# A gate product that keeps its place in program order on VectorE

## The chip, the core and the metric

The kernel runs on one core of a Trainium2 chip. A core has five engines that run their own instruction queues: TensorE (PE in the profile, its weight loads PEld), VectorE (DVE), ScalarE (ACT), GpSimd (POOL) and SyncE (SP). The metric is the device time of one launch in microseconds; lower is better.

## What is computed

The reference is one decoder layer on x of 512 tokens by 1024 channels, in float32: a mixer (projections, two causal convolutions, a linear recurrence, gates), and then a feed-forward part that picks, for every token, 16 of 16384 experts per head with 8 heads. Only the second part touches the change:

```python
def peer(n, w_q, sub_keys_1, sub_keys_2, expert_u, expert_v):
    ...
        g = jax.nn.softmax(top_s, axis=-1)
        u_sel = jnp.take(expert_u, idx, axis=0)
        act = jax.nn.gelu(jnp.einsum('thkd,td->thk', u_sel, xc).astype(jnp.float32))
        v_sel = jnp.take(expert_v, idx, axis=0)
        return jnp.einsum('thk,thkd->td', (g * act).astype(xc.dtype), v_sel)
    ...
    h = h + peer(n, w_q[l], sub_keys_1[l], sub_keys_2[l], expert_u[l], expert_v[l])
    return rms_norm(h, norm_final)
```

## The kernel before, in words

For 384 of the 512 tokens the kernel does not gather experts. It computes gelu(U n) for all 16384 experts, in 128 tiles of 128 experts, multiplies each tile by a dense matrix of gates (zero where an expert was not chosen), and accumulates the product with V in PSUM. The last 128 tokens go by gathered rows: 128 indirect DMAs, each bringing one expert row (u and v) per token, with two VectorE instructions each (L410 for the dot product, L397 for the sum).

Every matmul is done in three passes with high and low parts. A weight tile of 128x1024 is loaded on SP's queue (`raw`, 4 buffers), ScalarE rounds it into `whi` (L75) and VectorE subtracts to get `wlo` (L76).

The stages are: the mixer, the search for the top experts, the building of the gate matrix (written to a DRAM scratch `gscr`), and last the expert stage, the loop over j from 0 to 128 at the end of `layer`. The change touches only that last stage.

An activation tile comes from one of two places. 52 of the 128 tiles are computed in the loop itself by `act_tile` (24 matmuls, L90; the gelu at L378 writes tile `gel`). The other 76, listed in `LAG`, were computed in earlier stages: 12 of them wait in SBUF (`keep`), 64 were written to DRAM (`ascr`) and are read back in the loop (`back`, 6 buffers) by DMAs on ScalarE's queue (L673), requested three tiles ahead.

`out_tile(j, g)` then does, for the tile before the current one: reads of gates for the next eight tiles (`gt`, two buffers, four DMAs per group of eight tiles on ScalarE's queue, L637); the load and the splitting of V (`weights`); the product of activations and gates on VectorE (L650); the splitting of that product into `w_hi` (ScalarE, L75) and `w_lo` (VectorE, L76), two buffers each; and 18 matmuls (L657), in which `w_hi` times `whi` comes first, `w_hi` times `wlo` second, and `w_lo` times `whi` third.

What sets the order on each engine is a scheduler in the framework: it takes the instructions in the order in which they become ready by its own estimate, within the limits of buffers and data. A call of `tc.keep_in_program_order` takes an instruction out of that freedom: it stays in the written order among all others so marked. Marked already are the two VectorE instructions of a gathered row and the DMAs of `gt` and `back`. Within an engine the built order is then fixed, and each instruction starts only when the one before it has started and its own waits are over.

Of the kernel before, what the change touches and what calls it, by code (L numbers as in the profile page):

```python
# [35 lines left out]
TG = 32  # L36
# [20 lines left out]
def layer(ctx: ExitStack, tc: tile.TileContext, a):  # L57
    nc = tc.nc
    V, A, G, T, SP = nc.vector, nc.scalar, nc.gpsimd, nc.tensor, nc.sync
# [12 lines left out]
    def split(raw, shape, tags, pool, bufs, lo_eng=None):  # L72
        hi = pool.tile(shape, F32R, tag=tags[0], name=tags[0], bufs=bufs)
        lo = pool.tile(shape, F32R, tag=tags[1], name=tags[1], bufs=bufs)
        A.activation(hi, raw, AF.Copy)  # L75
        (lo_eng or V).tensor_sub(lo, raw, hi.bitcast(F32))  # L76
        return hi, lo

    def weights(src, k, eng=None):
        raw = ring.tile([P, k * P], F32, tag="raw", name="raw", bufs=4)  # L80
        SP.dma_start(raw, src)
        hi, lo = split(raw, [P, k * P], ("whi", "wlo"), ring, 3, eng)
        return hi.rearrange("p (k m) -> p k m", k=k), lo.rearrange("p (k m) -> p k m", k=k)
# [65 lines left out]
    with tc.tile_pool(name="mix", bufs=1) as mp:  # L149
# [64 lines left out]
        for j in range(KR):  # L214
# [16 lines left out]
            c = next(columns)  # L231
            held[c] = proj(c, COLS)
            gates = []
            for s, bname, tag in ((0, "brg", "lr"), (1, "big", "lx")):
# [3 lines left out]
                gt = mp.tile([P, S], F32, tag=tag, name=tag, bufs=KR)  # L238
# [131 lines left out]
    def act_tile(j):  # L370
        u = weights(a["ut"][j], KD, G if j in LAG[:AR + AD] else V)
        pa = bank("01", (P, S))
        mm3(pa[:, :ND], u, n2d)
        if j in LAG[:JK]:
            g = gp.tile([P, ND], F32, tag="keep", name="keep", bufs=JK)
        else:
            g = gp.tile([P, ND], F32, tag="gel", name="gel", bufs=3)
        A.activation(g, pa[:, :ND], AF.Gelu_apprx_tanh)  # L378
        return g
# [42 lines left out]
    with tc.tile_pool(name="top", bufs=1) as rp:  # L422
# [114 lines left out]
        for t in range(NT):  # L537
            g, sel = decode(t)
# [13 lines left out]
    with tc.tile_pool(name="gates", bufs=1) as rp:  # L552
# [19 lines left out]
        for n, (t, t0) in enumerate(blocks):  # L572
# [3 lines left out]
            c, s0 = divmod(t0, TG)  # L576
# [54 lines left out]
    def read_gates(n, c0, c1):  # L631

        if n * JG >= P:
            return
        if c0 == 0:
            gst[n] = ep.tile([P, NG, JG, TG], F32, tag="gt", name="gt", bufs=2)
        tc.keep_in_program_order(A.dma_start(gst[n][:, c0:c1], gscr[c0:c1, :, n * JG : (n + 1) * JG, :].rearrange("c p j t -> p c j t")))  # L637

    def out_tile(j, g):
        nonlocal nout  # L640
        k = j % JG
        if j == 0:
            for c in range(0, NG, 2):
                read_gates(0, c, c + 2)
        if 3 <= k < 7:
            read_gates(j // JG + 1, 3 * k - 9, 3 * k - 6)
        gt = gst[j // JG][:, :, k, :]
        v = weights(a["uv"][j * P : (j + 1) * P, D:], KD, V)
        vf = [x.rearrange("p k m -> p (k m)") for x in v]
        V.tensor_mul(g.rearrange("p (c t) -> p c t", t=TG), g.rearrange("p (c t) -> p c t", t=TG), gt)  # L650
        w = split(g, [P, ND], ("w_hi", "w_lo"), ep, 2)
        passes = [(x, y, f) for x, y in ((0, 0), (0, 1), (1, 0)) for f in range(2)]
        if nout == P - 1:
            passes.sort(key=lambda p: p[2])
        for t in range(NT):
            for x, y, f in passes:
                T.matmul(  # L657
                    acc[t][f],
                    w[x][:, t * P : (t + 1) * P],
                    vf[y][:, f * S : (f + 1) * S],  # L660
                    start=nout == 0 and (x, y) == (0, 0),
                    stop=nout == P - 1 and (x, y) == (1, 0),
                    skip_group_check=True,
                )
        nout += 1
# [17 lines left out]
    for j in range(P + 1):  # L683
        if j < P:
            read_back(j + PRE)
            g = kept[j] if j in LAG else act_tile(j)
            part += share[j]
        if prev is not None:
            out_tile(*prev)
        if 8 <= j < 8 + 2 * KD and j % 2 == 0:  # L690
            residual(j // 2 - 4)
        prev = (j, g)
        while done < min(len(work), math.ceil(part * len(work) / total)):
            work[done]()
            done += 1
# [54 lines left out]
```

## Time and profile before

| | |
|---|---|
| median of 3 runs | 1806.83 us (1806.39 to 1808.25) |
| the profiled execution | 1811.19 us |
| its span, first to last instruction | 1809.5 us |
| PE busy in the span | 1738.8 us |
| VectorE busy in the span | 1287.9 us |
| expert stage, 1012 to 1797 us | 785 us, PE busy 753.37 us |

The profile is one execution, so sums are made against its span. Idle time of an engine counts only where the end waits for it. In the rows further down a PE row with brackets names how long PE stood idle before it, and what it was released by.

### The profile page before, as it was taken

The page shows a single profiled execution, that of the slowest core. Times are in us where ns is not written, and L with a number is a line of the kernel's source. Part 1 is how long each engine was busy: PE and PEld are TensorE (multiplying, and loading weights), DVE is VectorE, ACT ScalarE, POOL GpSimd, SP SyncE. Part 2 cuts the span into 40 slices and gives each one's busy share as a digit, 9 for nine tenths or more (in the row PEclk, how much of TensorE's full clock was granted, in tenths as well). Part 3 has the DMA queues.
Part 4 walks back from the last instruction along what each step waited for, and adds up shares of the span by engine and source line. Part 5 has one row for each costly group of instructions (what it writes and reads, how often), then busy time and mean ns, then how long its engine had stood idle before and what let it go on. Part 6 is the DMA issues. An engine that isn't in the chain of part 4 may idle for free. (4 is left out here: it accounts for less than half of the span.)

```text
span 1809.5 us, 23987 instructions
## 1 busy us (share of the span) xinstructions
PE 1738.8 (96%) x8861; PEld 1515.1 (84%) x8861; DVE 1287.9 (71%) x2341; ACT 765.6 (42%) x1290; POOL 386.9 (21%) x257
## 2 busy tenths in 40 slices
PE   8999999999989998999999899999899999989998
PEld 6888888888878887999999788888787887878886
DVE  8969442225578669999996676777777876767774
ACT  5774332222343336455554333443333433434353
POOL 0000000000145555022685112122121221112200
PEclk9999999999999999999999999999999999999999
DMA  4323223333433335589999897898898897878872
GB/s 167 125 79 103 94 86 93 102 105 99 138 105 103 105 119 195 168 319 370 351 361 372 308 324 275 324 356 318 287 331 307 320 335 274 333 280 315 308 238 90
DMA packets 124246, 410.85 MB, mean 227 GB/s; under 512 B 12128, under 2 KB 55392, under 8 KB 106080
## 3 DMA queue, kind: packets, MB, share of 16 engines
q1 hardware_dynamic: 59904, 199.58, 33.1%
q0 software_dynamic: 18432, 134.23, 19.2%
q10 hardware_dynamic: 45792, 75.51, 11.5%
q8 instruction: 69, 1.13, 0.2%
q14 instruction: 49, 0.40, 0.1%
HBM read 367.33 MB, written 41.94 MB: 226 GB/s over the span
## 5 line engine op out<-in xcount | busy, mean ns | idle before, releaser
L75 ACT ACTIVATE whi<-raw 128x1024 fp32r<-128x1024 f32 (+1 forms) x364 | 380.1, 1046 | 601.5 <-PE ps L90 388.3
L76 DVE TENSOR_TENSOR wlo<-raw,whi 128x1024 fp32r<-128x1024 f32 (+1 forms) x324 | 387.9, 1199 | 237.0 <-ACT whi L75 236.5
L90 PE MATMUL ps<-q_hi,whi 128*128 128x384 f32 (+1 forms) x1232 | 435.5, 353 | 14.6 <-ACT whi L75 10.3
L90 PE MATMUL ps<-q_hi,wlo 128*128 128x384 f32 (+1 forms) x1232 | 429.5, 349 | 2.0 <-DVE wlo L76 2.0
L90 PE MATMUL ps<-q_lo,whi 128*128 128x384 f32 (+1 forms) x1232 | 429.0, 348 | 0.3 <-DVE q_lo L144 0.3
L403 POOL DMA_INDIRECT row<-uv,uidx x128 | 262.9, 2054 | 716.9 <-DVE yg L397 712.2
L657 PE MATMUL acc<-whi,w_hi 128*128 128x512 f32 x768 | 245.3, 401 | 29.7 <-ACT w_hi L75 25.4
L90 PEld LDWEIGHTS ps<-q_hi,whi 128*128 128x128 f32 x1232 | 234.3, 190 | 27.4 <-ACT whi L75 11.6
L657 PE MATMUL acc<-whi,w_lo 128*128 128x512 f32 x768 | 243.3, 398 | 6.2 <-DVE w_lo L76 6.2
L90 PEld LDWEIGHTS ps<-q_hi,wlo 128*128 128x128 f32 x1232 | 233.5, 190 | 13.8 <-DVE wlo L76 4.8
L90 PEld LDWEIGHTS ps<-q_lo,whi 128*128 128x128 f32 x1232 | 234.1, 190 | 10.9 <-DVE q_lo L144 0.7
L657 PE MATMUL acc<-wlo,w_hi 128*128 128x512 f32 x768 | 242.3, 397 | 0.0
L657 PEld LDWEIGHTS acc<-whi,w_hi 128*128 128x128 f32 x768 | 145.7, 193 | 62.3 <-ACT w_hi L75 31.7
L657 PEld LDWEIGHTS acc<-whi,w_lo 128*128 128x128 f32 x768 | 147.5, 193 | 39.3 <-DVE w_lo L76 7.9
L76 POOL TENSOR_TENSOR wlo<-raw,whi 128x1024 fp32r<-128x1024 f32 x40 | 98.5, 2466 | 357.1 <-ACT whi L75 357.1
L657 PEld LDWEIGHTS acc<-wlo,w_hi 128*128 128x128 f32 x768 | 147.2, 192 | 32.0
L90 PE MATMUL ps<-n_hi,whi 128*128 128x512 f32 x432 | 168.4, 390 | 0.0
L90 PE MATMUL ps<-n_hi,wlo 128*128 128x512 f32 x432 | 168.2, 390 | 0.0
L90 PE MATMUL ps<-n_lo,whi 128*128 128x512 f32 x432 | 168.1, 389 | 0.0
L397 DVE SCALAR_TENSOR_TENSOR yg<-row,dots,yg 128x1024 f32<-128x1024 f32 x128 | 163.5, 1278 | 0.0
L410 DVE SCALAR_TENSOR_TENSOR junk<-row,n2tok 128x1024 bf16<-128x1024 f32 x128 | 155.6, 1216 | 0.0
L90 PEld LDWEIGHTS ps<-n_hi,wlo 128*128 128x128 f32 x432 | 81.1, 188 | 17.5 <-DVE wlo L76 0.4
(204 smaller groups left out, 1902.0 us busy)
## 6 DMA issues: line engine op xcount, KB each, us to landing
raw<-ut SPq DMA_DIRECT2D x128, 512.0 KB
raw<-uv SPq DMA_DIRECT2D x128, 512.0 KB
raw<-w_in SPq DMA_DIRECT2D x60, 512.0 KB
gscr<-stg ACTq DMA_DIRECT2D x12, 2048.0 KB
gt<-gscr ACTq DMA_DIRECT2D x60, 384.0 KB
ascr<-gel ACTq DMA_DIRECT2D x64, 192.0 KB
back<-ascr ACTq DMA_DIRECT2D x64, 192.0 KB
raw<-w_q SPq DMA_DIRECT2D x16, 512.0 KB
```

The lines of the kernel that those rows point to most:

```text
L75: A.activation(hi, raw, AF.Copy)
L76: (lo_eng or V).tensor_sub(lo, raw, hi.bitcast(F32))
L90: T.matmul(ps, w[x][:, i, :], r[y][i], start=first and n == 0, stop=last and n == 3 * k - 1)
L397: V.scalar_tensor_tensor(yg, r[:, D:], dots[:, i : i + 1], yg, op0=ALU.mult, op1=ALU.add)
L403: ins = G.indirect_dma_start(out=r, out_offset=None, in_=a["uv"], in_offset=bass.IndirectOffsetOnAxis(ap=uidx[:, i : i + 1], axis=0))
L410: V.scalar_tensor_tensor(junk, r[:, :D], 1.0, n2tok, op0=ALU.mult, op1=ALU.mult, accum_out=dots[:, i : i + 1])
L657: T.matmul(acc[t][f], w[x][:, t * P : (t + 1) * P], vf[y][:, f * S : (f + 1) * S], start=nout == 0 and (x, y) == (0, 0), stop=nout == P - ...
```

## The change

The product moves two lines up, ahead of `weights` for V of the same tile, and is marked to keep its place in program order.

```diff
         gt = gst[j // JG][:, :, k, :]
+        gv = g.rearrange("p (c t) -> p c t", t=TG)
+        tc.keep_in_program_order(V.tensor_mul(gv, gv, gt))
         v = weights(a["uv"][j * P : (j + 1) * P, D:], KD, V)
         vf = [x.rearrange("p k m -> p (k m)") for x in v]
-        V.tensor_mul(g.rearrange("p (c t) -> p c t", t=TG), g.rearrange("p (c t) -> p c t", t=TG), gt)
         w = split(g, [P, ND], ("w_hi", "w_lo"), ep, 2)
```

No instruction is added or removed. The order of PE, POOL and SP stays the same but for line numbers; VectorE and ScalarE are reordered within the expert stage. In the rows, `wlo` belongs to a weight tile, `w_lo` to a product; the product is L650 before and L649 after.

VectorE, before, around tile 42 (`gel_11506`) of the 128; `back_11544` is the activation of tile 46:

```order
L76 TENSOR_TENSOR w_lo_11516<-back_11297,w_hi_11515 128x384
L410 SCALAR_TENSOR_TENSOR junk_11539,dots_3822<-row_11537,n2tok_3823 128x1024
L397 SCALAR_TENSOR_TENSOR yg_3824<-row_11468,dots_3822,yg_3824 128x1024
L76 TENSOR_TENSOR wlo_11549<-raw_11546,whi_11548 128x1024
L650 TENSOR_TENSOR back_11544<-back_11544,gt_11189 128x384
L76 TENSOR_TENSOR wlo_11580<-raw_11577,whi_11579 128x1024
L650 TENSOR_TENSOR gel_11506<-gel_11506,gt_11189 128x384
L76 TENSOR_TENSOR w_lo_11554<-gel_11506,w_hi_11553 128x384
```

The same place on VectorE after the change:

```order
L410 SCALAR_TENSOR_TENSOR junk_11539,dots_3822<-row_11537,n2tok_3823 128x1024
L397 SCALAR_TENSOR_TENSOR yg_3824<-row_11468,dots_3822,yg_3824 128x1024
L76 TENSOR_TENSOR wlo_11550<-raw_11547,whi_11549 128x1024
L76 TENSOR_TENSOR wlo_11581<-raw_11578,whi_11580 128x1024
L649 TENSOR_TENSOR gel_11506<-gel_11506,gt_11189 128x384
L76 TENSOR_TENSOR w_lo_11554<-gel_11506,w_hi_11553 128x384
L649 TENSOR_TENSOR back_11366<-back_11366,gt_11189 128x384
L76 TENSOR_TENSOR w_lo_11585<-back_11366,w_hi_11584 128x384
```

The product of tile 46 no longer stands ahead of that of tile 42 (it is 15 rows behind it now), and that of tile 43 stands directly ahead of its own `w_lo`.

VectorE, before, around tiles 94 (`gel_14110`), 95 (`back_13974`) and 96 (`back_14047`), which is the first of a new group of gates (`gt_14009`):

```order
L650 TENSOR_TENSOR gel_14110<-gel_14110,gt_13614 128x384
L76 TENSOR_TENSOR w_lo_14167<-gel_14110,w_hi_14166 128x384
L650 TENSOR_TENSOR back_14047<-back_14047,gt_14009 128x384
L76 TENSOR_TENSOR w_lo_14196<-back_13974,w_hi_14195 128x384
L410 SCALAR_TENSOR_TENSOR junk_14219,dots_3822<-row_14217,n2tok_3823 128x1024
```

The same place on VectorE after the change:

```order
L649 TENSOR_TENSOR gel_14110<-gel_14110,gt_13614 128x384
L76 TENSOR_TENSOR w_lo_14167<-gel_14110,w_hi_14166 128x384
L649 TENSOR_TENSOR back_13974<-back_13974,gt_13614 128x384
L76 TENSOR_TENSOR wlo_14229<-raw_14226,whi_14228 128x1024
L76 TENSOR_TENSOR w_lo_14196<-back_13974,w_hi_14195 128x384
L410 SCALAR_TENSOR_TENSOR junk_14219,dots_3822<-row_14217,n2tok_3823 128x1024
L397 SCALAR_TENSOR_TENSOR yg_3824<-row_14149,dots_3822,yg_3824 128x1024
L649 TENSOR_TENSOR back_14047<-back_14047,gt_14009 128x384
```

The product of tile 96 has moved behind the `w_lo` of tile 95 and behind the two instructions of a gathered row.

## Rows read from the trace of the kernel before

**Rows 1.** Page, part 1: engine, busy us (share), instructions.

```profile
PE 1738.8 (96%) x8861; PEld 1515.1 (84%) x8861; DVE 1287.9 (71%) x2341; ACT 765.6 (42%) x1290; POOL 386.9 (21%) x257
```

**Rows 2.** Windows: stretch, length, busy PE PEld DVE ACT POOL, PEclk, DMA share, GB/s.

```profile
1012.00:1797.00 785.00, 753.37 (x3536) 652.22 (x3537) 576.10 (x743) 314.25 (x566) 146.97 (x100) 0.98 0.83 298
1166.00:1222.00 56.00, 56.00 (x271) 49.15 (x271) 45.56 (x59) 23.85 (x44) 13.02 (x9) 1.00 0.93 341
```

**Rows 3.** Waits, 1012 to 1797: waiter <- releaser: us, times, longest.

```profile
DVE back L650 <- DMA back<-ascr: 43.3, 21, 4.7
...
PE acc L657 <- ACT w_hi L75: 25.4, 15, 2.9
DVE back L650 <- DMA gt<-gscr: 22.6, 5, 8.9
...
PE acc L657 <- DVE w_lo L76: 6.2, 3, 4.7
...
PE acc L657 <- issue: 4.4, 1, 4.4
```

**Rows 4.** Timeline of DVE around tile 42: start, us, instruction [idle before <-releaser].

```profile
1266.43 0.56 DVE L650 TENSOR_TENSOR back<-back,gt 128x384 f32<-128x384 f32 x1 [4.72 <-DMA back<-ascr]
1266.91 1.22 DVE L76 TENSOR_TENSOR wlo<-raw,whi 128x1024 fp32r<-128x1024 f32 x1
1268.04 0.55 DVE L650 TENSOR_TENSOR gel<-gel,gt 128x384 f32<-128x384 f32 x1
```

**Rows 5.** Timeline of ACT, the gelu of tile 42.

```profile
1263.14 0.47 ACT L378 ACTIVATE gel<-ps 128x384 f32<-128x384 f32 x1
```

**Rows 6.** Timeline of PE, seven of the eighteen stalls by operands.

```profile
1106.28 0.74 PE L657 MATMUL acc<-whi,w_hi 128*128 128x512 f32 x2 [2.67 <-ACT w_hi L75]
...
1269.20 1.22 PE L657 MATMUL acc<-whi,w_hi 128*128 128x512 f32 x2 [2.80 <-ACT w_hi L75]
...
1306.68 1.22 PE L657 MATMUL acc<-whi,w_hi 128*128 128x512 f32 x2 [2.88 <-ACT w_hi L75]
...
1364.67 1.22 PE L657 MATMUL acc<-whi,w_hi 128*128 128x512 f32 x2 [2.78 <-ACT w_hi L75]
...
1503.56 0.73 PE L657 MATMUL acc<-whi,w_hi 128*128 128x512 f32 x2 [2.78 <-ACT w_hi L75]
...
1600.91 1.22 PE L657 MATMUL acc<-whi,w_lo 128*128 128x512 f32 x2 [4.72 <-DVE w_lo L76]
...
1708.47 0.73 PE L657 MATMUL acc<-whi,w_hi 128*128 128x512 f32 x2 [2.08 <-ACT w_hi L75]
```

**Rows 7.** Timeline of DVE, tiles 56 to 61.

```profile
1356.14 1.49 DVE L650 TENSOR_TENSOR back<-back,gt 128x384 f32<-128x384 f32 x3 [3.40 <-issue]
...
1361.90 0.56 DVE L650 TENSOR_TENSOR back<-back,gt 128x384 f32<-128x384 f32 x1 [0.32 <-DMA back<-ascr]
```

**Rows 8.** Chain that ended last: start, us, what.

```profile
1378.85 8.17 PE acc L657 x36
...
1492.66 9.71 DMA gt<-gscr
...
1587.16 12.55 DMA gt<-gscr
```

**Rows 9.** Windows of 4 us behind two stalls, columns as in rows 2.

```profile
1268.00:1272.00 4.00, 2.80 (x7) 2.22 (x8) 3.41 (x7) 2.46 (x5) 0.00 (x0) 0.62 0.71 258
...
1600.00:1604.00 4.00, 3.09 (x7) 2.48 (x8) 4.00 (x6) 1.78 (x4) 0.53 (x1) 0.51 0.15 39
1604.00:1608.00 4.00, 4.00 (x14) 3.32 (x13) 4.00 (x6) 1.49 (x4) 1.15 (x1) 0.64 0.66 174
```

**Rows 10.** Timeline of DVE, tiles 45 and 46, where PE does not wait.

```profile
1286.54 0.56 DVE L76 TENSOR_TENSOR w_lo<-gel,w_hi 128x384 fp32r<-128x384 f32 x1 [0.59 <-ACT w_hi L75]
...
1290.49 0.56 DVE L76 TENSOR_TENSOR w_lo<-back,w_hi 128x384 fp32r<-128x384 f32 x1
```

**Rows 11.** Timeline of PE, the first matmuls of tile 45.

```profile
1287.22 0.62 PE L657 MATMUL acc<-whi,w_hi 128*128 128x512 f32 x2
```

## Prediction

> **What bounds the kernel now.** I read the page first, then the waits of the last stage, then the timelines around its stalls. PE is busy 96% of the span [rows 1], so what can be won is PE's idle time and what follows from it. In the expert stage, 1012 to 1797 us, PE is busy 753 of 785 us [rows 2]. The waits of that stage name the missing part [rows 3]: PE's matmuls L657 wait 15 times for `w_hi` (25.4 us), 3 times for `w_lo` (6.2 us), and once 4.4 us at the start of the stage, where the first gates are loaded. The last one stays: nothing there changes. The other 31.6 us are what the change can reach.
>
> Both `w_hi` and `w_lo` come from the product, and the product's engine stands still for DMAs: VectorE waits 21 times, 43.3 us in all, for `back`, and 5 times, 22.6 us, for `gt` [rows 3]. How that gets to PE is seen at tile 42. Its gelu begins at 1263.14 and takes 0.47 [rows 5]. But the product of tile 46 stands ahead on VectorE and waits 4.72 us for its `back` [rows 4]; tile 42's own product runs only at 1268.04, and PE stands idle 2.80 us until 1269.20 [rows 6]. Tile 46 is needed four tiles later. So a wait for data that nobody needs yet blocks, on an in-order queue, data that PE needs now.
>
> **What the change removes.** It puts each product behind all that VectorE must do for earlier tiles. In the built order no product of `back` or `keep` stands ahead of the product of an earlier tile, and PE's order is the same. A `back` tile then has its product asked for when its own tile is next, several tiles after its DMA was issued. So the waits for `back` should vanish from the path. I went through the 18 stalls by the product that waited ahead of them.
>
> - Four stalls are at the first tile of a group of gates which PE reaches straight after other product tiles: 2.67, 2.88, 2.78 and 2.08 us at 1106, 1306, 1503 and 1708 [rows 6]. Here the tile itself needs the gates that have not landed. The order doesn't help, since the gate reads keep their places on ScalarE. 10.4 us stay.
> - At 1364.67 there are 2.78 us [rows 6], partly for the same reason: VectorE stood still until 1356.14 for tile 56, the first of its group, and then had work queued up [rows 7]. Before, three products ran there (1.49 us) and later one more waited 0.32 and ran 0.48 (as the first row of [rows 4] holds up the second). After, two of the three (1.0) and the last with its wait (0.8) are elsewhere, but the `wlo` of tile 56, formerly done during the wait, now stands behind the product: 1.13, the distance of two rows of [rows 4]. 2.78 - 1.0 - 0.8 + 1.13 = 2.1 us stay.
> - The rest goes: 31.6 - 10.4 - 2.1 = 19.1 us. The largest is the 4.72 at 1600.91 [rows 6], where the product of tile 96, waiting for new gates, blocked the `w_lo` of tile 95 in the middle of tile 95's matmuls. After the change that `w_lo` is ahead of it, and PE has the rest of tile 95 and the 24 matmuls of an activation tile to do until it wants tile 96. The stall of 2.80 at 1269.20 is the second.
>
> **The clock behind the stalls.** Behind a long stall PE runs slow for a while: the granted clock is 0.62 in the 4 us from 1268, and 0.51 and 0.64 in the 8 us from 1600 [rows 9], against 1.00 in a stretch without a stall [rows 2]. [...] The work lost is (1 - 0.62) x 4 = 1.5 us at the first, (0.49 + 0.36) x 4 = 3.4 us at the second. Both stalls go, so 4.9 us come back. For the stalls that stay, and for the one at 1364, I credit nothing.
>
> **What it costs.** The product itself is no new work: 128 of them, 0.55 us each [rows 4], as before. What is new is that the product of a kept tile stands behind the two instructions of a gathered row and ahead of `w_lo`. In a stretch without stalls the `w_lo` of tile 45 starts at 1286.54 and that of tile 46 at 1290.49, 3.95 later, with a gathered row and a `wlo` between [rows 10]. With a product of 0.48 it is 4.43, against 4.09 that PE takes for a tile (8.17 for two, [rows 8]). But VectorE is ahead: `w_lo` of tile 45 starts 0.68 before PE's first matmul of that tile, at 1287.22 [rows 11], and PE uses `w_lo` only in the third pass, behind four matmuls, 0.9 us in. So the next `w_lo` ends at 1286.54 + 4.43 + 0.56 = 1291.53, and is wanted at 1287.22 + 4.09 + 0.9 = 1292.21. I take this at zero; PE's own work hides it with 0.7 us to spare. Its bounds are zero and the second rival.
>
> ScalarE's queue has `w_hi` in order too: a `w_hi` that waits for a later product holds up the `whi` and the DMA issues behind it. The scheduler moved those `w_hi` back by some places, and the gate reads stand where they stood but for one place at a time. I take zero.
>
> The faster pace also loads the DMA engines more. They are busy 0.83 of the stage, and 0.93 in a stretch without stalls [rows 2]; a gate read lands 9.7 us after its issue, once 12.55 [rows 8]. At the four group starts that stay a later landing is lost one for one. I take 0.5 us each, 2 us, with bounds of 0 and 3 us each (12.55 against 9.7).
>
> [...]
>
> **The sum.** 19.1 + 4.9 - 2 = 22 us. The span goes from 1809.5 to 1787.5; the execution, 1.7 us longer than its span, from 1811.2 to 1789.2; and since the median lies 4.4 us below the profiled execution, the median to 1784.8. I say 1785, 1.2% faster.
>
> **The rivals.**
>
> *Gates become the bound.* The stalls for `back` go, but loads bunch up and the gate reads land later: the four stalls grow by 3 us each, to 1795; and if some of the other group starts that PE now passes without waiting begin to stall as well, to about 1801. For it: DMA at 0.93 without stalls, and gate reads issued only some 10 us before they are used. Against it: most group starts have an activation tile of 24 matmuls ahead of them on PE.
>
> *Products just in time (slower).* Each of the 52 computed tiles is followed on PE by a tile whose product was ready long before. Now it is made within one tile of PE's time. If VectorE is late by more than the 0.7 us worked out above, every such place loses what the product adds, 0.55 us: 52 x 0.55 = 29 us against the 22 that are won, so 1785 + 29 = 1814. It decides at the first `w_lo` behind a computed tile. Against it: VectorE is busy 576 of 785 us in the stage [rows 2].
>
> *Nothing changes in sum.* The stalls are only moved: PE waits for the gates at the next group start for as long as it saved before, since the loads behind are no faster. That would be 1803 to 1810. Against it: the DMA engines are idle 17% of the stage [rows 2], after stalls most of all (0.15 of the time from 1600, [rows 9]).
>
> *More than I think.* Gate reads land earlier because VectorE frees buffers evenly: half of the 10.4 us and its slow clock go too, below 1776.
>
> **How the numbers follow.** Forecast, 1775 to 1795: 0.63. Gates become the bound, 1795 to 1803: 0.20. More than I think: 0.03. Nothing in sum: 0.06. Slower: 0.08. A measurement of this kernel tells about 0.2%, 3.6 us, from no change. So faster is 0.63 + 0.20 + 0.03 = 0.86, same 0.06, slower 0.08. The range of 8 in 10 takes the forecast with its bounds and most of the first rival: 1772 to 1801.
>
> **What would show it.** Right: VectorE's waits for `back` fall from 43 us to a few; PE's waits for `w_hi` and `w_lo` fall from 31.6 to about 13, and stand at the first tiles of groups; the granted clock no longer falls around tiles 42 and 95. Wrong: many short stalls of PE for `w_lo` behind computed tiles (the second rival), or waits for `gt` that grew past 30 us (the first).

## The result, and the profile after

| | before | after |
|---|---|---|
| median of 6 runs | 1809.38 us (1806.39 to 1814.81) | 1785.84 us (1781.47 to 1790.10) |
| the profiled execution | 1811.19 us | 1786.26 us |
| its span | 1809.5 us | 1784.5 us |

The ratio is 0.9867, 95% interval 0.9845 to 0.9889: the change is 1.3% faster. The forecast was 1785 us, in a range from 1772 to 1801.

VectorE does the same work in the same time (1287.9 us before, 1287.8 after). PE's busy time fell from 1738.8 [rows 1] to 1728.9 us, although it runs the same matmuls. Page of the changed kernel, part 1, columns as in rows 1:

```profile
PE 1728.9 (97%) x8861; PEld 1509.5 (85%) x8861; DVE 1287.8 (72%) x2341; ACT 764.2 (43%) x1290; POOL 325.2 (18%) x257
```

Nearly the whole difference lies in the expert stage: 24.2 of the 25.0 us by which the span is shorter. Windows from PE's first matmul of the stage to the end of the span, columns as in rows 2, first of the kernel before and then of the changed one:

```profile
1012.11:1809.50 797.39, 757.24 (x3552) 655.06 (x3552) 581.00 (x755) 320.02 (x581) 146.97 (x100) 0.98 0.82 295
```

```profile
1011.35:1784.50 773.15, 748.82 (x3552) 651.61 (x3552) 580.77 (x755) 318.89 (x581) 145.99 (x100) 0.98 0.85 304
```

Of the 24.2 us, 8.4 us are PE's busy time (757.24 - 748.82), and the remaining 15.8 us are its idle time. The waits say where the idle time went. Waits of the changed kernel from 1012 us to the end, which answer to [rows 3] (waiter <- releaser: us, times, longest):

```profile
DVE back L649 <- DMA gt<-gscr: 26.8, 6, 6.9
...
PE acc L658 <- ACT w_hi L75: 15.8, 7, 3.7
...
PE acc L658 <- issue: 4.8, 1, 4.8
DVE back L649 <- DMA back<-ascr: 2.2, 1, 2.2
```

VectorE's waits for `back` are down from 21 with 43.3 us to one with 2.2. PE waited 18 times, 31.6 us, for `w_hi` and `w_lo`, and now waits 7 times, 15.8 us, for `w_hi` alone; there is no row of PE waiting for `w_lo` any more. VectorE's waits for `gt` grew from 22.6 to 26.8 us, but most of that is a change of name: its wait at tile 56, the first of a group, stood under `issue` with 3.40 us before [rows 7], and stands under `gt` with 4.96 now.

In the built order of the kernel before, 58 of the 128 products stand ahead of the product of an earlier tile; in the changed one a single one does, that of tile 2 ahead of tile 1.

Five of the seven stalls that are left are the ones that the prediction left. Timeline of PE after (start, us, instruction, in brackets the idle time before it), the five longest, which answer to [rows 6]:

```profile
1105.14 0.73 PE L658 MATMUL acc<-whi,w_hi 128*128 128x512 f32 x2 [2.50 <-ACT w_hi L75]
...
1296.82 0.73 PE L658 MATMUL acc<-whi,w_hi 128*128 128x512 f32 x2 [2.72 <-ACT w_hi L75]
...
1354.72 0.73 PE L658 MATMUL acc<-whi,w_hi 128*128 128x512 f32 x2 [2.18 <-ACT w_hi L75]
...
1491.74 0.80 PE L658 MATMUL acc<-whi,w_hi 128*128 128x512 f32 x2 [3.69 <-ACT w_hi L75]
...
1683.76 1.22 PE L658 MATMUL acc<-whi,w_hi 128*128 128x512 f32 x2 [3.39 <-ACT w_hi L75]
```

The place of the longest stall before, tile 95 in front of the new group at tile 96, shows the mechanism. Timeline of VectorE after:

```profile
1576.06 0.55 DVE L649 TENSOR_TENSOR back<-back,gt 128x384 f32<-128x384 f32 x1
...
1578.71 0.55 DVE L76 TENSOR_TENSOR w_lo<-back,w_hi 128x384 fp32r<-128x384 f32 x1
...
1585.98 0.56 DVE L649 TENSOR_TENSOR back<-back,gt 128x384 f32<-128x384 f32 x1 [4.37 <-DMA gt<-gscr]
```

VectorE still stands 4.37 us at the product of tile 96 until its gates land. But the `w_lo` of tile 95 (1578.71) is now in front of that wait and not behind it, and PE has no stall there.

### The profile page after: what moved, and what is told of

It is laid out like the page before. It is cut to its first block, busy times and chain, and to the rows that moved or that the text cites. A ratio compares the mean times of both kernels' runs of the same rounds, so it can differ in the third digit from the quotient of the medians.

```text
span 1784.5 us, 23972 instructions
## 1 busy us (share of the span) xinstructions
PE 1728.9 (97%) x8861; PEld 1509.5 (85%) x8861; DVE 1287.8 (72%) x2341; ACT 764.2 (43%) x1290; POOL 325.2 (18%) x257
## 3 DMA queue, kind: packets, MB, share of 16 engines
q10 hardware_dynamic: 45792, 75.51, 11.8%
## 4 chain that ended last, share of the span: by engine, by line
PE 77%; DVE 11%; DMA 6%; issue 4%; ACT 1%; POOL 1%; SPq 0%; DVEq 0%; POOLq 0%; ACTq 0%
PE ps L90 48%; PE acc L658 26%; DMA gt<-gscr 4%; DVE wlo L76 2%; DVE ehl L567 2%; DVE e L565 1%; DMA row<-uv,uidx 1%; DVE yg L397 1%; DVE junk L410 1%; PE ps L518 1%; PE ps L237 1%; POOL row L403 1%; DMA raw<-ut 1%; DVE nk L142 1%; DMA raw<-w_in 0%
## 5 line engine op out<-in xcount | busy, mean ns | idle before, releaser
L403 POOL DMA_INDIRECT row<-uv,uidx x128 | 201.4, 1573 | 752.2 <-DVE yg L397 747.6
L658 PE MATMUL acc<-whi,w_hi 128*128 128x512 f32 x768 | 242.4, 396 | 20.6 <-ACT w_hi L75 15.8
L658 PEld LDWEIGHTS acc<-whi,w_lo 128*128 128x128 f32 x768 | 146.1, 191 | 31.7 <-DVE w_lo L76 0.7
```

The source lines that it names most:

```text
L403: ins = G.indirect_dma_start(out=r, out_offset=None, in_=a["uv"], in_offset=bass.IndirectOffsetOnAxis(ap=uidx[:, i : i + 1], axis=0))
L658: T.matmul(acc[t][f], w[x][:, t * P : (t + 1) * P], vf[y][:, f * S : (f + 1) * S], start=nout == 0 and (x, y) == (0, 0), stop=nout == P - ...
```

## The experiments

All runs of one group shared the runs of the kernel before: 1811.27 us in the first group (e1, e2, e4, e5), 1811.74 in the second (e3, e8 and the two of e6). The ratio of the changed kernel is against its own 1809.38. The stage length is taken as above, from the profiled execution.

| kernel | median us | ratio to before | expert stage us |
|---|---|---|---|
| before | | | 797.4 |
| after | 1785.84 | 0.9867 (0.9845 to 0.9889) | 773.2 |
| e1_moved_free | 1814.04 | 1.0009 (0.9983 to 1.0035) | 805.7 |
| e2_pinned_late | 1792.25 | 0.9892 (0.9842 to 0.9941) | 783.0 |
| e3_before_back5 | 1807.91 | 0.9979 (0.9958 to 0.9999) | 793.5 |
| e4_after_gt2 | 1760.86 | 0.9732 (0.9685 to 0.9779) | 748.4 |
| e8_pinned_late_gt2 | 1761.46 | 0.9708 (0.9667 to 0.9748) | 748.2 |
| e5_before_gt2 | 1840.32 | 1.0172 (1.0105 to 1.0239) | 819.3 |
| e6_extra1 | 1772.63 | 0.9780 (0.9741 to 0.9819) | 758.7 |
| e6_extra2 | 1798.90 | 0.9923 (0.9900 to 0.9947) | 782.8 |

### Which half of the change does it: the place or the order?

The change moves the product up and takes it out of the scheduler's hands. Each half alone:

```diff
# e1_moved_free, against the kernel before
+        gv = g.rearrange("p (c t) -> p c t", t=TG)
+        V.tensor_mul(gv, gv, gt)
         v = weights(a["uv"][j * P : (j + 1) * P, D:], KD, V)
         vf = [x.rearrange("p k m -> p (k m)") for x in v]
-        V.tensor_mul(g.rearrange("p (c t) -> p c t", t=TG), g.rearrange("p (c t) -> p c t", t=TG), gt)
```

```diff
# e2_pinned_late, against the kernel before
         vf = [x.rearrange("p k m -> p (k m)") for x in v]
-        V.tensor_mul(g.rearrange("p (c t) -> p c t", t=TG), g.rearrange("p (c t) -> p c t", t=TG), gt)
+        gv = g.rearrange("p (c t) -> p c t", t=TG)
+        tc.keep_in_program_order(V.tensor_mul(gv, gv, gt))
```

> The product is moved ahead of the splitting of V as in the changed kernel, but not marked to keep its place. In the built order VectorE again runs products of later tiles ahead (that of tile 46 stands ahead of that of tile 42). My theory, that the gain comes from later products no longer blocking the queue: no gain, within 0.3% of the kernel before (about 1807), VectorE's waits for back again some 40 us. Rival, that the two lines of moving are what helps (the product earlier than the splitting of its own V): about 1786, as the changed kernel.

> The product stays where it was written, behind the loading and splitting of V, but is marked to keep its place in program order. My theory: nearly the whole gain, 1784 to 1790, VectorE's waits for back below 5 us. Rival, that the place ahead of the splitting is needed (a product behind wlo comes too late for w_hi): some short waits of PE for w_hi, 1795 to 1807.

Moved up but left free, the product gains nothing: 1.0009, an interval that holds 1. In the built order 58 products again stand ahead of an earlier tile's, and the waits are of the same kinds as before: for `back` 36.6 us against 43.3, and PE's for `w_hi` and `w_lo` 37.1 against 31.6. Waits of e1_moved_free from 1012 to 1797 us:

```profile
DVE back L649 <- DMA back<-ascr: 36.6, 15, 4.8
...
PE acc L658 <- ACT w_hi L75: 30.5, 16, 5.8
DVE back L649 <- DMA gt<-gscr: 27.3, 6, 9.3
...
PE acc L658 <- DVE w_lo L76: 6.6, 3, 5.1
```

Kept in order at its old place, it gains nearly all: 1792.25 us, a little above the expected range. Waits of e2_pinned_late, same stretch:

```profile
DVE back L651 <- DMA gt<-gscr: 29.7, 6, 8.2
...
PE acc L658 <- ACT w_hi L75: 23.5, 10, 7.3
DVE back L651 <- DMA raw<-uv: 7.1, 2, 4.4
```

No wait for `back` is left, and PE waits for no `w_lo`. What is left of PE's waits is for gates: the longest, 7.31 us at 1692.92, follows a product that stood 8.17 us for `gt`. The view names `raw` for three of VectorE's waits (the two of the last row, and one of 2.9 us at 1246.48), but a product reads no `raw`, and all three stand at the first tile of a group (40, 56 and 96). So the order is what works. Whether the 6 us between this kernel and the changed one are real these runs cannot say, since the two intervals overlap; e8 below asks again.

### Was only the lead of the transfer too short?

If the rows in `back` were simply read too late, an earlier read would do the same as the order. The kernel before, with its products free:

```diff
# e3_before_back5, against the kernel before
-PRE = 3
+PRE = 5
...
-            kept[j] = ep.tile([P, ND], F32, tag="back", name="back", bufs=6)
+            kept[j] = ep.tile([P, ND], F32, tag="back", name="back", bufs=8)
```

> The kernel before, with the transposed rows read back five tiles ahead instead of three and eight buffers for them instead of six; the products stay free. Theory (the rows are late because the products of later tiles stand ahead of earlier ones, and so hold the row buffers and wait in front): the products are free to go further ahead in turn with more buffers, VectorE still waits for the rows in the expert stage (over 15 us in total), and the time stays within 1795 to 1830 us. Rival (only the lead of the transfer was too short): VectorE's waits for the rows go below 5 us, and the time comes to about 1786 us, as in the changed kernel.

The time is the theory's, 1807.91 us, 0.2% under before; the waits are between the two. Waits of e3_before_back5, 1012 to 1797 us:

```profile
DVE back L650 <- DMA gt<-gscr: 34.7, 8, 9.0
...
PE acc L657 <- ACT w_hi L75: 23.9, 12, 4.3
DVE back L650 <- DMA back<-ascr: 10.9, 6, 2.8
...
PE acc L657 <- DVE w_lo L76: 5.6, 2, 4.8
```

The waits for `back` fell from 43.3 to 10.9 us, below the 15 that the theory had named, so the earlier read does help there. But PE's waits only went from 31.6 to 29.5 us, because the waits for `gt` rose from 22.6 (26.0 with the 3.40 that stood under `issue`) to 34.7: a product with its row at hand goes ahead and waits for its gates instead. In the built order 58 of the 128 products of this kernel still stand ahead of the product of an earlier tile, as many as before. Taking away one wait of an operation that stands too early let it run into the next one here.

### The stalls that are left: are they the gates?

The prediction put four of the five long stalls down to gates that land late. In the next three kernels the four gate reads of a group are issued two tiles earlier:

```diff
# e4_after_gt2 against the changed kernel, e8_pinned_late_gt2 against e2, e5_before_gt2 against the kernel before
-        if 3 <= k < 7:
-            read_gates(j // JG + 1, 3 * k - 9, 3 * k - 6)
+        if 1 <= k < 5:
+            read_gates(j // JG + 1, 3 * k - 3, 3 * k)
```

> The changed kernel, with the gates of the next group read two tiles earlier (from the second tile of a group on rather than from the fourth). What is left in the changed kernel are 15.8 us of PE waiting for w_hi at the first tiles of groups, all behind VectorE's waits for gt, and slow clock behind them. My theory: these waits go too; 15.8 us and some 7 us of slow clock, 1762 to 1768. Rival, that the DMA engines are the bound by now: the gates land later in step, the waits stay or move to the weights, 1780 to 1787.

> The product kept in program order at its old place, behind the splitting of V, with the earlier gate reads as well. Theory (the place ahead of the splitting is worth little beside the order; what the late-placed kernel lacked at 1792 us is its waits for gates): about 1761 us, 1758 to 1766. Rival (the place itself is worth some 6 us): 1767 us or more, with TensorE's waits for w_hi left in the expert stage.

> The kernel before, with the gates read two tiles earlier as in e4, and the product free as before. My theory: the stalls at group starts go (some 12 us and their slow clock, some 8), those behind waits for back stay (some 10 us and their slow clock): 1788 to 1796, VectorE's waits for back still about 40 us. Rival, that the waits for gt were what made the products of back tiles late: the waits for back go as well, 1770 or less.

With the order kept, the earlier reads take away every stall of PE in the stage but the one at its start. The stage of e4_after_gt2, as windows (columns as in rows 2), and PE's only stall by the timeline:

```profile
1008.33:1756.70 748.37, 739.79 (x3552) 647.72 (x3552) 580.54 (x755) 318.18 (x581) 147.47 (x100) 0.99 0.87 314
```

```profile
1008.33 1.19 PE L658 MATMUL acc<-whi,w_hi 128*128 128x512 f32 x2 [5.15 <-issue]
```

1760.86 us, a little under the expected range, is 2.7% under before, and faster than the changed kernel. The gates do not travel faster: page, part 6 of e4_after_gt2 and of e2_pinned_late, whose reads are at the old place (tile<-scratch, engine, times, KB each, median us from issue to landing):

```profile
gt<-gscr ACTq DMA_DIRECT2D x60, 384.0 KB, 9.4
```

```profile
gt<-gscr ACTq DMA_DIRECT2D x60, 384.0 KB, 9.5
```

They only start earlier. e8 gives 1761.46 us, the same as e4: with the gates early, the place ahead of the splitting of V or behind it makes no difference that these runs can tell. So what e2 lost against the changed kernel were waits for gates.

The kernel before with the same edit missed its expectation altogether: it is 1.7% slower, 1840.32 us. Waits of e5_before_gt2, 1012 to 1797 us:

```profile
DVE back L650 <- DMA back<-ascr: 74.3, 29, 5.9
...
DVE back L650 <- DMA gt<-gscr: 46.0, 7, 9.5
...
PE acc L657 <- ACT w_hi L75: 33.7, 21, 4.3
...
PE acc L657 <- DVE wlo L76: 7.4, 2, 3.9
```

VectorE's waits for `back` and for `gt`, 120.3 us, are nearly twice those before (65.9), though the gates are asked for earlier. The built order tells why: with the next group's gates read early, the scheduler puts 30 products of a new group ahead of products of the group still in use, where before it put none. One such wait reaches PE as follows. Timeline of VectorE, and of PE, in e5_before_gt2:

```profile
1197.52 0.56 DVE L650 TENSOR_TENSOR back<-back,gt 128x384 f32<-128x384 f32 x1 [9.48 <-DMA gt<-gscr]
...
1199.61 1.22 DVE L76 TENSOR_TENSOR wlo<-raw,whi 128x1024 fp32r<-128x1024 f32 x1
```

```profile
1200.88 1.22 PE L657 MATMUL acc<-wlo,w_hi 128*128 128x512 f32 x2 [3.85 <-DVE wlo L76]
```

This is the product of tile 32, the first of its group, and it stands ahead of that of tile 30. It waits 9.48 us for its gates, the `wlo` three instructions behind it comes late, and PE loses 3.85 us. So the two edits are not independent: the earlier gates are worth 25 us with the order kept, and cost 29 us without it.

### How much room has VectorE?

The rival on the slower side rested on the room that the product has before PE wants it; the prediction took 0.7 us per tile. e4, the fastest kernel, with one or two products more, of the same size, ahead of each tile's own (they write a scratch tile that nothing reads):

```diff
# e6_extra1 (range(1)) and e6_extra2 (range(2)), against e4_after_gt2
         gv = g.rearrange("p (c t) -> p c t", t=TG)
+        for _ in range(1):
+            scr = ep.tile([P, ND], F32, tag="scr", name="scr", bufs=1)
+            tc.keep_in_program_order(V.tensor_mul(scr.rearrange("p (c t) -> p c t", t=TG), gv, gt))
         tc.keep_in_program_order(V.tensor_mul(gv, gv, gt))
```

> The changed kernel with earlier gate reads (1760.9 us in its run), with one more product of the same size (0.48 us) on VectorE right ahead of each tile's product, into a scratch tile. Theory (VectorE has some 0.7 us to spare between a tile's two parts of the splitting and TensorE's need): the time stays at 1761 to 1769 us, with few new waits of TensorE. Rival (nothing to spare, the product is just in time): 52 products x 0.48 = 25 us more, some 1786 us, with TensorE's waits for w_hi in most tiles.

> As the last, with two more products (0.96 us) ahead of each tile's product. Theory (0.7 us to spare): 0.26 us come through in each of 52 tiles, some 14 us, so 1770 to 1790 us, with waits of TensorE for w_hi or w_lo that were not there with one. Rival (nothing to spare): 52 x 0.96 = 50 us, some 1811 us; if the spare is well over 1 us: still under 1770 us.

One product more costs 11.8 us (1772.63 against 1760.86), two cost 38.0. Both miss the theory's ranges on the high side, and both stay under the rival's prices of 25 and 50. So there is room, but less than 0.7 us. It shows on PE's weight loads, which wait for `w_hi`. Waits of PEld in e6_extra1, 1012 to 1757 us:

```profile
PEld acc L661 <- ACT w_hi L75: 11.4, 40, 0.9
...
PEld acc L661 <- DVE w_lo L76: 3.7, 16, 0.3
```

In e4 there is one such wait for `w_hi`, of 0.3 us, and none for `w_lo`. The stage grew by 10.4 us (758.73 - 748.37), or 0.20 us for each of the 52 computed tiles, so the room comes out as 0.48 - 0.20 = 0.28 us. That is an estimate, which takes the loss as if it were spread evenly over those tiles. The kernel with two gives nearly the same, 0.96 - 34.4 / 52 = 0.30, but there VectorE is busy 56.49 of 60 us in the middle of the stage (1200 to 1260), and a bound by its sum of work cannot be told from a chain that is too long. Besides, the built order of PE, which is the same in all other kernels here, changed in these two: in some places matmuls of an activation tile moved ahead of those of an output tile. So the added product is not the only thing that differs from e4.

The trace of e4 shows the room at a computed tile directly: its product on VectorE, its `w_hi` on ScalarE, and PE's load of it (timelines of the three engines):

```profile
1281.96 0.55 DVE L649 TENSOR_TENSOR gel<-gel,gt 128x384 f32<-128x384 f32 x1
```

```profile
1282.55 0.53 ACT L75 ACTIVATE w_hi<-gel 128x384 fp32r<-128x384 f32 x1 [1.39 <-DVE gel L649]
```

```profile
1283.57 0.41 PEld L658 LDWEIGHTS acc<-whi,w_hi 128*128 128x128 f32 x2
```

`w_hi` ends at 1283.08, and PE loads it at 1283.57: 0.49 us, which is also the median of the 52 computed tiles. At the tile behind it the same distance is 0.61 us, and 0.47 us for its `w_lo`. These are larger than the 0.28 us of the estimate; how the loss spreads over the tiles is not shown.

## Why the prediction was right, point by point

*The stalls that go.* 31.6 us were to fall to 14.5 (10.4 at four group starts, 2 more there for later gates, 2.1 at tile 57). They fell to 15.8. The four group starts lost 2.50 + 2.72 + 3.69 + 3.39 = 12.3 us, where 12.4 was forecast, and the one at 1354.72 lost 2.18 where 2.1 was forecast. Two short ones of 0.31 and 0.98 us, at 1547.38 and 1593.83, were not in the sum; ahead of each VectorE had waited for gates (2.74 us at 1539.53, 4.37 at 1585.98) and then had work queued up. So the first rival, gates that become the bound, came true for about a microsecond.

*That four stalls are the gates'* was read from the trace of before alone; e4 shows it, since with gates read two tiles earlier they are gone, and the one at tile 57 with them.

*Later gates.* The four starts lost 1.9 us more than before (12.3 against 10.4), with 2 forecast, but not 0.5 each: 2.67, 2.88, 2.78 and 2.08 us became 2.50, 2.72, 3.69 and 3.39. At the third the gate read took 9.71 us from issue to landing before [rows 8] and 10.63 after, 0.92 more, and the stall grew by 0.91; at the fourth it took 9.02 and 10.32, 1.30 more, and the stall grew by 1.31. So at these two the later landing was lost one for one, as forecast. Chain that ended last, the fourth start before, then the third and the fourth after:

```profile
1698.26 9.02 DMA gt<-gscr
```

```profile
1479.92 10.63 DMA gt<-gscr
...
1672.24 10.32 DMA gt<-gscr
```

That the faster pace made them land later is not shown, since the first two starts lost a little less than before. What was measured is that the DMA share of the stage rose from 0.82 to 0.85, and that the gates landed later at two of the four starts. The 3 us at each start that the first rival named were far too high: 1.9 us were lost at the four together.

*The clock* is the term that was sized too small: 4.9 us were credited, and PE's busy time fell by 8.4. The two places named are at a granted clock of 1.00 now. Windows after, around the former stall of tile 42 and behind tile 95 (columns as in rows 9):

```profile
1260.00:1264.00 4.00, 4.00 (x19) 3.34 (x18) 2.94 (x6) 2.04 (x4) 0.00 (x0) 1.00 1.00 401
...
1580.00:1588.00 8.00, 8.00 (x42) 7.22 (x41) 3.63 (x6) 2.79 (x5) 0.94 (x1) 1.00 0.94 340
```

The prediction credited nothing at the stalls that stay. But at one of them, at 1503.56, the clock had been lower than at the others, 0.57 over 8 us, and the stall at the same place after is followed by 0.79: another (0.79 - 0.57) x 8 = 1.8 us. The two windows, before and after (columns as in rows 9):

```profile
1503.56:1511.56 8.00, 7.32 (x19) 5.39 (x20) 8.00 (x11) 2.15 (x5) 1.68 (x1) 0.57 0.47 127
```

```profile
1491.74:1499.74 8.00, 8.00 (x31) 6.77 (x32) 8.00 (x12) 3.31 (x7) 1.01 (x1) 0.79 0.63 204
```

Why it had been lower there is not shown. A second, short wait of PE for `w_lo` (0.68 us) stood right behind that stall before and is gone after, but one of 0.77 us stood behind the stall at 1106.28 too, where the clock was 0.79. The 1.7 us that still lack are not traced to a place.

*What it costs.* Zero was right for this kernel, since no new wait of PE for `w_lo` appeared. But the 0.7 us of room was too much. The working measured to PE's matmul, while PE takes `w_hi` and `w_lo` in the weight load ahead of it (in the stage before, PEld waited 16 times, 31.7 us, for `w_hi` and 4 times, 7.9 us, for `w_lo`), which begins 0.22 us earlier: at 1287.00 for the first matmul of tile 45, which begins at 1287.22 [rows 11]. Timeline of PEld before:

```profile
1287.00 0.41 PEld L657 LDWEIGHTS acc<-whi,w_hi 128*128 128x128 f32 x2
```

With that, 0.68 becomes 0.46 us, and 0.47 is what the `w_lo` of the tile behind a computed one has in e4. It also looked at `w_lo` alone, while `w_hi`, which the first pass wants, has 0.49 us at the computed tile and is what most loads wait for in e6_extra1. The rival of products just in time was therefore nearer than its working had it.

*Nothing in sum* fell: PE's idle time at group starts took back 3 us of it (1.9 and the two short stalls), not all.

*The sum* was 22 us on the span, and 25.0 came: 1.3 less from the stalls, 3.5 more from the clock, and 0.8 ahead of the stage, which was not in the sum. That the median, 1785.84, agrees with the 1785 of the forecast to 1 us is luck: the span was 3 us shorter than forecast, but the median lies only 0.4 us below the profiled execution, where 4.4 was taken.

## What to carry to other kernels

An operation on an engine that works in order, as VectorE did here, should not be allowed to run ahead of what is needed sooner, however ready it seems: what counts is not how long it waits but who stands behind it. In e5 a wait of 9.48 us had a `wlo` behind it that PE needed, and PE lost 3.85; in e3 VectorE's waits for `back` and `gt` were 45.6 us against 65.9 before, and PE's waits still 29.5 against 31.6. Fix the order first and then move the loads earlier; the same earlier loads made the kernel 1.7% slower while the order was free, and 1.4% faster once it was fixed. To see how much room a chain has, add a known piece of work to it and read which wait appears first; look also whether the scheduler left the rest of the order alone.

## What the runs showed of the hardware

A stall of PE of 2.08 us or more cost more than its own length here: in the 8 us behind it the mean granted clock was 0.57 to 0.81, against 1.00 in a stretch without a stall [rows 2]. Windows of 8 us from the end of stalls in the kernel before, of 2.67, 1.59, 1.66 and 2.08 us, columns as in rows 9:

```profile
1106.28:1114.28 8.00, 7.22 (x25) 5.68 (x26) 8.00 (x11) 2.71 (x7) 1.68 (x1) 0.79 0.54 164
...
1455.33:1463.33 8.00, 8.00 (x40) 7.26 (x41) 6.26 (x8) 2.87 (x5) 0.94 (x1) 1.00 0.70 233
...
1673.27:1681.27 8.00, 8.00 (x35) 6.65 (x36) 7.97 (x11) 3.82 (x8) 1.01 (x1) 1.00 0.79 278
1708.47:1716.47 8.00, 8.00 (x31) 6.63 (x32) 8.00 (x13) 3.42 (x7) 1.68 (x1) 0.79 0.71 213
```

The granted clock is the third number from the end: 0.79, 1.00, 1.00, 0.79; a mean below 1.00 took in a stretch at 0.50. Behind the stall at 1354.72 in the changed kernel, with a mean of 0.79 over 8 us, windows of 1 us show 1.00 in the first, 0.50 in the next three, 0.79 in the fifth and 1.00 in the last three. In both kernels the mean was 0.57 to 0.81 behind every stall of 2.08 us or more in the stage, and 1.00 behind each of up to 1.66 us, but for short waits right behind a long stall. A mean of 0.79 over 8 us is 1.7 us of work lost, beside the stall. Over the stage, 31.6 us less idle time, from before to e4, came with 17.4 us less busy time (757.24 - 739.79): in the mean, each microsecond of stall cost 1.55. The windows of 8 us behind the seven stalls of 2.08 us or more before account for 14.6 of the 17.4 us, at a granted clock of 0.57 to 0.80.
